# Two more tile pairs in a seven-product form, and its weight sums moved from VectorE to accumulating DMA

## The chip, the core and the metric

The kernel runs on one core of one Trainium2 chip. The metric is device time in microseconds of the whole launch. Three runs of the kernel before gave 1008.6, 1009.3 and 1009.34 us, so 1009.3 us is the median. One more run was profiled.

The engines have these names in the profile: PE is TensorE (matrix products; PEld is its weight load), DVE is VectorE (elementwise work), ACT is ScalarE (copies, casts and activation functions), POOL is GpSimd, which here issues DMAs and does little else, and SP is SyncE, which issues most of the weight loads.

## The reference

One layer of a decoder trunk over 512 tokens of width 1024, in float32. Cut to what matters here:

```python
h = rmsnorm(x, norm_mix_g)
proj = h @ w_in                       # 10 sections of 512 columns, then 3 x 1024 gate columns
...
branches = jnp.stack([conv_out, sb_out, ret_out], axis=2)
up = jnp.einsum('bsnw,nwd->bsnd', branches, w_branch)
gates = jax.nn.sigmoid(gate_logits.reshape(b, s, 3, 1024) + b_gate)
merged = jnp.sum(gates * up, axis=2)
x = x + merged @ w_o
```

After this come a cross-attention into 256 memory tokens and a squared-ReLU MLP, each with a residual add. The change is in `gates`: 24 tiles of 128 gate columns (three branches of eight), each a product of a 1024 x 128 block of `w_in` with the 1024 x 512 transpose of `h`.

## The kernel before

**Products.** Every float32 operand is split into a high and a low part (`parts_of` for weights, `split` for activations): the high part is a cast on ACT, the low part the difference to it, taken on DVE. Each product is then three matmuls, high by high, high by low and low by high (`mm3`, L362 to L364). A plain gate tile (`gates`, L1002) is 8 blocks of 128 rows by 3 matmuls of 512 columns, 24 in all. It is followed by the branch's own projection (`proj_t` with `nk=4`, 12 matmuls of 512 columns), a sigmoid on ACT and, on DVE, a multiplication and, for the second and third branch, an addition (`gated`, L986).

**The seven-product form** (`gates7`, `item_t7`, `seven`) takes two gate tiles at a time. Their weight, 1024 rows by 256 columns, is cut into four blocks B11, B12, B22 and B21 of 512 x 128. The activations are cut into four blocks by rows and token halves. Instead of eight block products with 512 rows and 256 tokens there are seven, of sums of blocks, as in the fast matrix multiplication of Strassen and Winograd. One product is 4 x 3 matmuls of 256 columns (L420), so a pair takes 84 matmuls of 256 columns instead of 48 of 512. The products use a PSUM bank several times over: `seven` runs A11·B11, S1·T1, S2·T2, A12·B21, S3·T3, S4·B22 and A22·T4 in this order, and between them copies partial results out on ACT (L426, L428, L430) or adds them on DVE (L432, L434, L436). So the third product waits until the first result has been copied out of its bank. S1 to S4 are sums of activation blocks, made once (`Mixes`); T1 to T4 are sums of weight blocks, made anew for each pair.

**Weights** stream through two rings. A load on SP's queue brings 128 x 1024 floats (512 KB) into one of six raw buffers (`w_raw`, `RAWS`). A *step* of a weight entry turns a raw buffer into high and low parts in `w_part`, ten buffers (`WBUFS`). Where a part has 512 columns, high and low share one buffer. A plain entry has one step. The class `Seven` has two loads, raw[0] with B11 | B12 and raw[1] with B22 | B21, and four steps: s0 makes the parts of B11; s1 forms T1 and T3 in place by two DVE operations of 512 columns (L129, L132) and makes their parts; s2 forms T2 and T4 by two more and makes theirs; s3 makes the parts of B22 and B21. This takes seven `w_part` buffers. `AHEAD = 2` steps are traced ahead of the item that needs them. The classes `Wide`, `Early` and `Summed` do the same for other matrices; two of them already let a DMA add one weight block to another (`add`, L235 to L237: a DMA of 512 KB issued by POOL, with `accum_op=ALU.add`).

**Order.** The kernel is traced as a list of items (`plan`). A planner then decides the order of instructions on each engine from costs that it assumes; at run time each engine takes its instructions in that fixed order, and waits come from semaphores. Only a few stretches keep the traced order.

**Which tiles.** `G7 = 12, G8 = 20`: of the 24 gate tiles, 12 to 19 are done in the seven-product form (two pairs of the second branch, two pairs of the third); the last four, tiles 4 to 7 of the third branch, are plain. Each two finished tiles of the third branch are made ready for the output projection on ACT and DVE by `Pairs.make` (L448). The output projection `w_o` follows (`items_w`, L494; steps of the class `Early`, which uses DVE for the sums of its stages P5 and P6 and one DMA add). Its stages P1, P2 and P5 come once for the first half of the merged tiles (j = 0) and once for the second (j = 1), then P6.

**Room for activations** is a pool of 30 units of 128 x 1024 floats. `Mixes` holds eight of them until the last seven-product pair has used them. The reload of `x` (L101, four units, issued on POOL in traced order) waits for free units.

Of the kernel before, what the change touches and what calls it, by code (L numbers as in the profile page):

```python
# [13 lines left out]
ALU = mybir.AluOpType  # L14

P = 128
# [15 lines left out]
C_N = 44  # L32
UNITS, SCRS = 30, 9
RAWS, WBUFS, AHEAD = 6, 10, 2
G7, G8, UP = 12, 20, 8


@with_exitstack
def trunk_kernel(ctx: ExitStack, tc: tile.TileContext, x, mem, par, rot, dqd, kdec, g_mix, g_xa, g_mem, g_mlp,
# [91 lines left out]
    def plus(out, a, b):  # L131
        dve.tensor_tensor(out=out, in0=a, in1=b, op=ALU.add)  # L132

# [43 lines left out]
    class Seven:  # L177

        def __init__(self, t, c):
            self.loads = [(t, c), (t, c + 1)]
            self.need = (1, 2, 2, 2)
            self.steps = [self.s0, self.s1, self.s2, self.s3]
            self.parts = []

        def s0(self, raw):
            return parts_of(raw[0][:, :512])

        def s1(self, raw):  # L190
            l, r = raw[0][:, :512], raw[0][:, 512:]
            minus(l, r, l)
            plus(r, r, raw[1][:, :512])
            return parts_of(raw[0])

        def s2(self, raw):
            l, r = raw[0][:, :512], raw[0][:, 512:]
            plus(l, raw[1][:, :512], l)
            minus(r, raw[1][:, 512:], l)
            return parts_of(raw[0])  # L200

        def s3(self, raw):
            return parts_of(raw[1])

        def get(self):
            where = dict(B11=(0, 0), T1=(1, 0), T3=(1, 1), T2=(2, 0), T4=(2, 1), B22=(3, 0), B21=(3, 1))
            return {n: [w[:, o * 512:(o + 1) * 512].rearrange("p (a b) -> p a b", a=4) for w in self.parts[i]]
                    for n, (i, o) in where.items()}

# [168 lines left out]
    class Mixes:  # L378
# [7 lines left out]
        def make(self, g):  # L386

            def whole(k0, t0):
                x = scr("mix", (P, 2, 256))
                hi, lo = self.a.span(k0 + 2 * g, 2, slice(t0, t0 + 256))  # L390
                dve.tensor_tensor(out=x, in0=hi.bitcast(F32), in1=lo.bitcast(F32), op=ALU.add)
                return x

            def mix(n, out, x, y, op):
                dve.tensor_tensor(out=out, in0=x, in1=y, op=op)
                h, l = self.parts[n]
                split(h[:, 2 * g:2 * g + 2, :], l[:, 2 * g:2 * g + 2, :], out)

            a11, a21 = whole(0, 0), whole(0, 256)
            mix("S3", scr("mix", (P, 2, 256)), a21, a11, ALU.subtract)  # L400
            mix("S1", a21, a21, whole(4, 256), ALU.subtract)
            mix("S2", a11, a11, a21, ALU.subtract)
            a12 = whole(4, 0)
            mix("S4", a12, a12, a11, ALU.subtract)

        def __getitem__(self, n):
            if n[0] == "S":
# [4 lines left out]
    def seven(b, a):  # L412


        def prod(ps, an, bn, first):
            bh, bl = b[bn]
            for k in range(4):
                ah, al = a[an][k]
                for i, (x, y) in enumerate(((bh, ah), (bh, al), (bl, ah))):
                    te.matmul(ps[:, :256], x[:, k, :], y, start=first and k == 0 and i == 0,  # L420
                              stop=k == 3 and i == 2, skip_group_check=True)

        p1, p2, p3 = atps("p1"), mmps("p2"), atps("p3")
        s, u = scr("sv_s"), scr("sv_u")
        prod(p1, "A11", "B11", True)
        act.copy(out=s[:, LH], in_=p1[:, LH])  # L426
# [7 lines left out]
        dve.tensor_tensor(out=s[:, RH_], in0=p1[:, LH], in1=s[:, RH_], op=ALU.add)  # L434
        prod(p3, "S4", "B22", False)
        dve.tensor_tensor(out=u[:, RH_], in0=p3[:, LH], in1=u[:, RH_], op=ALU.add)  # L436
        prod(p1, "A22", "T4", False)
        return s, u, p1

    class Pairs:  # L440
# [7 lines left out]
        def make(self, e, s, u):  # L448

            def put(names, src):  # L450
                w = unit("pr", (P, 2, 2, 256))
                split(w[:, 0], w[:, 1], src)
                for i, n in enumerate(names):
                    self.w[e][n] = w[:, 0, i, :], w[:, 1, i, :]

            def neg(out, a, b):
                dve.scalar_tensor_tensor(out=out, in0=a, scalar=-1.0, in1=b, op0=ALU.mult, op1=ALU.subtract)
# [1049 lines left out]
```

## Time and profile before

| | before |
|---|---|
| three runs | 1008.6, 1009.3, 1009.34 us |
| profiled execution | 1008.65 us, of which 1006.9 us span |
| mean granted TensorE clock | 0.997 of full speed |
| PE busy | 989.5 us, 98% of the span |
| DVE busy | 716.9 us, 71% |
| ACT busy | 531.2 us, 53% |
| POOL busy | 73.7 us, 7% |
| DMA | 113.61 MB, mean 113 GB/s |

In a line of groups the columns are line, engine, operation, output and inputs by the program's names, shapes, count, then busy time and the mean duration of one in ns, then the idle time of the engine just before and what ended it. Matmuls are pipelined: the duration of one is longer than the spacing of two, so what matters for PE is the spacing, which the chain of waits gives as a sum over many. The seven-product matmuls (L420) start between 373.1 and 443.6 us from the start of the span; those of the output projection (L494) begin at 468.2 us.

### The profile page before, as it was taken

How to read it: one execution, taken by the hardware profiler on the slowest of the kernel's cores; microseconds unless marked ns; L12 is line 12 of the kernel's file. 1: busy time of each engine (PE TensorE's matmuls, PEld its weight loads, DVE VectorE, ACT ScalarE, POOL GpSimd, SP SyncE). 2: the span in 40 equal slices, each digit the busy share in tenths (PEclk: the TensorE clock that was granted, in tenths of full speed). 3: DMA queues.
4: the chain of work that ended last, by engine and by line, in shares of the span. 5: the costliest groups of instructions: out<-in, count | busy, mean ns of one | idle time of the engine just before them, and what ended most of it. 6: DMA issues, size and time to landing. Idle time of an engine off the chain costs nothing.

```text
span 1006.9 us, 13109 instructions
## 1 busy us (share of the span) xinstructions
PE 989.5 (98%) x4944; PEld 836.9 (83%) x4944; DVE 716.9 (71%) x1073; ACT 531.2 (53%) x913; POOL 73.7 (7%) x136
## 2 busy tenths in 40 slices
PE   7999999999999999999999999999999999999997
PEld 6788888878888889988798888889888888888885
DVE  5757787778463797778896457875785785695786
ACT  6456666766533244454664446546643553553544
POOL 1000111223010000001100001010000000000000
PEclk9999999999999999999999999999999999999998
DMA  9342222222222213435565335733044035215212
GB/s 353 135 141 84 84 85 98 91 84 84 63 84 84 85 27 99 145 128 188 146 219 179 92 90 112 187 127 104 2 148 155 32 104 169 62 46 186 83 42 84
DMA packets 32352, 113.61 MB, mean 113 GB/s; under 512 B 4000, under 2 KB 4000, under 8 KB 32288
## 3 DMA queue, kind: packets, MB, share of 16 engines
q1 hardware_dynamic: 28224, 99.65, 29.9%
q0 software_dynamic: 3056, 11.02, 4.7%
q10 hardware_dynamic: 1008, 2.10, 0.6%
q8 instruction: 39, 0.64, 0.3%
q14 instruction: 25, 0.20, 0.1%
HBM read 110.66 MB, written 2.10 MB: 112 GB/s over the span
## 4 chain that ended last, share of the span: by engine, by line
PE 92%; DVE 3%; DMA 2%; issue 1%; ACT 1%; POOL 0%; SPq 0%; POOLq 0%; DVEq 0%
PE mm L362 21%; PE mm L363 21%; PE mm L364 21%; PE p L494 20%; PE p L420 4%; DVE w_part L114 1%; PE o L815 1%; DMA x<-in_x_dram 1%; PE aT L781 1%; DMA w_raw<-in_w_in_dram 1%; PE z L757 0%; PE z L758 0%; PE at L596 0%; PE xsc L363 0%; PE xsc L364 0%
## 5 line engine op out<-in xcount | busy, mean ns | idle before, releaser
L113 ACT CAST w_part<-w_raw 128x1024 fp32r<-128x1024 f32 (+1 forms) x223 | 232.4, 1045 | 275.9 <-PE mm L363 128.9
L114 DVE TENSOR_TENSOR w_part<-w_raw,w_part 128x1024 fp32r<-128x1024 f32 (+1 forms) x223 | 269.9, 1213 | 143.9 <-ACT w_part L113 137.3
L362 PE MATMUL mm<-hT_h,w_part 128*128 128x512 f32 (+1 forms) x736 | 280.1, 383 | 1.8 <-DVE r_qk L878 1.2
L363 PE MATMUL mm<-hT_l,w_part 128*128 128x512 f32 (+1 forms) x736 | 280.8, 382 | 0.7 <-DVE hT_l L352 0.7
L364 PE MATMUL mm<-hT_h,w_part 128*128 128x512 f32 (+1 forms) x736 | 280.6, 382 | 0.0
L494 PE MATMUL p<-w_part,pr 128*128 128x512 f32 x864 | 201.9, 390 | 0.9 <-DVE w_part L114 0.4
L494 PEld LDWEIGHTS p<-w_part,pr 128*128 128x128 f32 x864 | 161.7, 188 | 36.2 <-DVE x L132 1.0
L362 PEld LDWEIGHTS mm<-hT_h,w_part 128*128 128x128 f32 x736 | 137.8, 188 | 28.0 <-DVE r_qk L878 1.9
L363 PEld LDWEIGHTS mm<-hT_l,w_part 128*128 128x128 f32 x736 | 138.6, 188 | 25.9 <-DVE hT_l L352 1.0
L364 PEld LDWEIGHTS mm<-hT_h,w_part 128*128 128x128 f32 x736 | 138.5, 188 | 25.7
L132 DVE TENSOR_TENSOR w_raw<-w_raw 128x1024 f32<-128x1024 f32 (+1 forms) x46 | 51.8, 1127 | 2.2 <-DMA w_raw<-in_w_o_dram 1.9
L129 DVE TENSOR_TENSOR x<-x,p 128x512 f32<-128x512 f32 x48 | 32.5, 683 | 12.1 <-PE p L494 12.0
L494 PE MATMUL p<-w_part,pr_b 128*128 128x512 f32 x144 | 34.8, 389 | 0.0
L769 DVE TENSOR_TENSOR_SCAN sb_suf<-ones,sb_e 128x128 f32<-128x128 f32 (+3 forms) x32 | 27.4, 857 | 9.6 <-POOL sb_e L748 8.3
L132 DVE TENSOR_TENSOR x<-x,p 128x512 f32<-128x512 f32 x36 | 24.0, 683 | 12.9 <-PE p L494 12.8
L494 PEld LDWEIGHTS p<-w_part,pr_b 128*128 128x128 f32 x144 | 27.0, 188 | 5.6
L772 ACT ACTIVATE sb_suf<-sb_suf 128x128 f32<-128x128 f32 (+3 forms) x32 | 15.1, 471 | 29.7 <-DVE sb_suf L771 29.5
L420 PE MATMUL p<-mix_h,w_part 128*128 128x256 f32 x128 | 25.0, 283 | 0.0
L565 ACT ACTIVATE xn<-x 128x512 f32<-128x512 f32 x24 | 15.1, 629 | 13.1 <-DVE x L129 6.1
L362 PE MATMUL mm<-w_part,xg_h 128*128 128x512 f32 x56 | 21.4, 391 | 0.6 <-DVE sb_v L357 0.6
L363 PE MATMUL mm<-w_part,xg_h 128*128 128x512 f32 x56 | 21.8, 389 | 0.0
L364 PE MATMUL mm<-w_part,xg_l 128*128 128x512 f32 x56 | 21.5, 389 | 0.0
(257 smaller groups left out, 1447.4 us busy)
## 6 DMA issues: line engine op xcount, KB each, us to landing
w_raw<-in_w_in_dram SPq DMA_DIRECT2D x55, 512.0 KB, 3.4
w_raw<-in_w_up_dram SPq DMA_DIRECT2D x32, 512.0 KB, 3.5
w_raw<-in_w_down_dram SPq DMA_DIRECT2D x32, 512.0 KB, 3.7
w_raw<-in_w_br_dram SPq DMA_DIRECT2D x12, 512.0 KB, 3.4
w_raw<-in_w_gate_dram SPq DMA_DIRECT2D x8, 512.0 KB, 3.3
w_raw<-in_w_o_dram SPq DMA_DIRECT2D x8, 512.0 KB, 4.2
w_raw<-in_w_xk_dram SPq DMA_DIRECT2D x8, 512.0 KB, 4.9
w_raw<-in_w_xv_dram SPq DMA_DIRECT2D x8, 512.0 KB, 4.0
```

What stands on the lines that cost most here:

```text
L113: act.copy(out=wh, in_=src)
L114: dve.tensor_tensor(out=wl, in0=src, in1=wh.bitcast(F32), op=ALU.subtract)
L129: dve.tensor_tensor(out=out, in0=a, in1=b, op=ALU.subtract)
L132: dve.tensor_tensor(out=out, in0=a, in1=b, op=ALU.add)
L362: te.matmul(ps, lh, rh, start=first, stop=False)
L363: te.matmul(ps, lh, rl, start=False, stop=False)
L364: te.matmul(ps, ll, rh, start=False, stop=last)
L420: te.matmul(ps[:, :256], x[:, k, :], y, start=first and k == 0 and i == 0, stop=k == 3 and i == 2, skip_group_check=True)
L494: te.matmul(acc[bank, i], x, y, start=p in ("P1", "P5", "P2") and j + k + m == 0, stop=j == 1 and k == 1 and m == 2, skip_group_check=True)
L565: act.activation(out=dst[:, cs], in_=src[:, cs], func=AF.Square, accum_out=ss[:, i:i + 1])
L769: dve.tensor_tensor_scan(out=suf[:, :s][:, ::-1], data0=ones[:, :s], data1=e1[:, :s][:, ::-1], initial=0.0, op0=ALU.mult, op1=ALU.add)
L772: act.activation(out=suf[:, :s], in_=suf[:, :s], func=AF.Exp)
```

## The change

The boundary `G8` goes from 20 to 24, so tiles 20 to 23 are done as two more pairs in the seven-product form: six pairs instead of four, and the host lays out these columns of `w_in` accordingly. In `Seven`, the four DVE operations that form T1 to T4 are replaced by four accumulating DMAs of 256 KB each, which POOL issues and which read the second block from HBM again. All T are plain sums now: T1 = B11 + B12, T3 = B12 + B22, T2 = T1 + B22, T4 = T2 + B21. So the signs of the activation sums and of two recombinations change; some subtractions and additions become a `scalar_tensor_tensor` that computes -a - b (`neg`). T2 and T4 are now made one after the other, so their parts are two steps of 512 columns instead of one of 1024; there are five steps, with the same seven buffers.

```diff
-G7, G8, UP = 12, 20, 8
+G7, G8, UP = 12, 24, 8
...
+    def neg(out, a, b):
+
+        dve.scalar_tensor_tensor(out=out, in0=a, scalar=-1.0, in1=b, op0=ALU.mult, op1=ALU.subtract)
...
         def __init__(self, t, c):
+            self.t, self.c = t, c
             self.loads = [(t, c), (t, c + 1)]
-            self.need = (1, 2, 2, 2)
-            self.steps = [self.s0, self.s1, self.s2, self.s3]
+            self.need = (1, 1, 1, 2, 2)
+            self.steps = [self.s0, self.s1, self.s2, self.s3, self.s4]
             self.parts = []
 
+        def add(self, raw, side, i, from_side):
+            cols = lambda h: slice(512 * h, 512 * h + 512)
+            pool.dma_start(out=raw[0][:, cols(side)], in_=self.t[self.c + i][:, cols(from_side)], accum_op=ALU.add)
+
         def s0(self, raw):
-            return parts_of(raw[0][:, :512])
+            parts = parts_of(raw[0][:, :512])
+            self.add(raw, 0, 0, 1)
+            self.add(raw, 1, 1, 0)
+            return parts
 
         def s1(self, raw):
-            l, r = raw[0][:, :512], raw[0][:, 512:]
-            minus(l, r, l)
-            plus(r, r, raw[1][:, :512])
-            return parts_of(raw[0])
+            parts = parts_of(raw[0])
+            self.add(raw, 0, 1, 0)
+            return parts
 
         def s2(self, raw):
-            l, r = raw[0][:, :512], raw[0][:, 512:]
-            plus(l, raw[1][:, :512], l)
-            minus(r, raw[1][:, 512:], l)
-            return parts_of(raw[0])
+            parts = parts_of(raw[0][:, :512])
+            self.add(raw, 0, 1, 1)
+            return parts
 
         def s3(self, raw):
             return parts_of(raw[1])
 
+        def s4(self, raw):
+            return parts_of(raw[0][:, :512])
+
         def get(self):
-            where = dict(B11=(0, 0), T1=(1, 0), T3=(1, 1), T2=(2, 0), T4=(2, 1), B22=(3, 0), B21=(3, 1))
+            where = dict(B11=(0, 0), T1=(1, 0), T3=(1, 1), T2=(2, 0), B22=(3, 0), B21=(3, 1), T4=(4, 0))
...
             a11, a21 = whole(0, 0), whole(0, 256)
-            mix("S3", scr("mix", (P, 2, 256)), a21, a11, ALU.subtract)
-            mix("S1", a21, a21, whole(4, 256), ALU.subtract)
-            mix("S2", a11, a11, a21, ALU.subtract)
+            mix("S3", scr("mix", (P, 2, 256)), a11, a21, minus)
+            mix("S1", a21, whole(4, 256), a21, minus)
+            mix("S2", a11, a11, a21, neg)
             a12 = whole(4, 0)
-            mix("S4", a12, a12, a11, ALU.subtract)
+            mix("S4", a12, a12, a11, neg)
...
         prod(p1, "S3", "T3", False)
-        dve.tensor_tensor(out=s[:, RH_], in0=p1[:, LH], in1=s[:, RH_], op=ALU.add)
+        neg(s[:, RH_], p1[:, LH], s[:, RH_])
         prod(p3, "S4", "B22", False)
-        dve.tensor_tensor(out=u[:, RH_], in0=p3[:, LH], in1=u[:, RH_], op=ALU.add)
+        neg(u[:, RH_], p3[:, LH], u[:, RH_])
```

More of the change, by code (lines that the diff above doesn't have):

```diff
@@ L394, in mix @@
             def mix(n, out, x, y, op):
-                dve.tensor_tensor(out=out, in0=x, in1=y, op=op)
+                op(out, x, y)
                 h, l = self.parts[n]
@@ L454, in put @@
                     self.w[e][n] = w[:, 0, i, :], w[:, 1, i, :]
-            def neg(out, a, b):
-                dve.scalar_tensor_tensor(out=out, in0=a, scalar=-1.0, in1=b, op0=ALU.mult, op1=ALU.subtract)
             v = scr("pr_v", (P, 2, 256))
```

## The prediction

> **What bounds the kernel now.** I read the page's totals first, then the chain that ended last.
>
> ```profile
> span 1006.9 us, 13109 instructions
> PE 989.5 (98%) x4944; PEld 836.9 (83%) x4944; DVE 716.9 (71%) x1073; ACT 531.2 (53%) x913; POOL 73.7 (7%) x136
> PE 92%; DVE 3%; DMA 2%; issue 1%; ACT 1%; POOL 0%; SPq 0%; POOLq 0%; DVEq 0%
> ```
>
> PE is busy for 98% of the span and makes up 92% of the chain. A saving elsewhere shows only where PE waits. The profiled execution took 1008.65 us, 1.75 us more than its span; the median of the three runs is 1009.3, 0.65 above it.
>
> Then the view of busy time by stretches, from where the last two pairs of the third branch begin to the output projection (columns: us, then PE, PEld, DVE, ACT and POOL, clock, DMA share, GB/s).
>
> ```profile
> 403.00:418.00 15.00, 15.00 (x108) 14.12 (x107) 10.48 (x15) 6.58 (x11) 0.00 (x0) 1.00 0.36 105
> 418.00:433.00 15.00, 15.00 (x93) 13.53 (x92) 12.38 (x18) 7.00 (x12) 0.00 (x0) 1.00 0.43 141
> 433.00:448.00 15.00, 15.00 (x87) 13.21 (x86) 8.71 (x12) 6.67 (x11) 0.75 (x1) 1.00 0.59 190
> 448.00:458.00 10.00, 10.00 (x46) 8.29 (x45) 9.84 (x15) 5.25 (x8) 0.56 (x1) 1.00 0.34 120
> 458.00:468.00 10.00, 10.00 (x45) 8.27 (x45) 7.95 (x11) 4.51 (x8) 3.75 (x7) 1.00 0.54 179
> 468.00:478.00 10.00, 10.00 (x46) 8.27 (x45) 9.31 (x12) 5.55 (x7) 0.00 (x0) 1.00 0.54 206
> 478.00:488.00 10.00, 9.91 (x44) 7.89 (x43) 9.91 (x14) 3.88 (x5) 2.33 (x3) 1.00 0.71 142
> ```
>
> PE has no gap before 478 us, the clock is full, and the DMA share stays under 0.75. DVE is the second limit, but only from 448 us on: 9.84 + 7.95 + 9.31 + 9.91 = 37.0 us of 40, so 3.0 us are free. In the 15 us before, 6.3 are free. The waits of the weight load between 366 and 520 us say what that does:
>
> ```profile
> PEld p L494 <- DVE w_part L114: 0.8, 1, 0.8
> PEld p L494 <- DVE x L129: 0.5, 1, 0.5
> PEld p L494 <- DVE x L132: 0.5, 1, 0.5
> PEld p L494 <- ACT w_part L113: 0.5, 1, 0.5
> ```
>
> All are in the output projection (L494), three of four end on DVE. The one on L132 is at 484.8 us; the others, 1.8 us together, lie behind 495 us. So the gate stage is bound by PE alone, and the handover to the output projection by PE and DVE together.
>
> **The change part by part. (1) Matmuls.** The spacing comes from the chain in order of time:
>
> ```profile
> 377.54 5.74 PE p L420 x48
> 442.47 1.43 PE p L420 x12
> 468.41 8.17 PE p L494 x36
> ```
>
> 256 columns cost 5.74/48 = 119.6 ns, 512 columns 8.17/36 = 226.9 ns. A pair of plain tiles is 48 x 226.9 = 10.89 us, a pair in seven products 84 x 119.6 = 10.05 us. That saves 0.85 us a pair and **1.7 us** for the two new pairs. Seven eighths of the arithmetic would have saved 1.36 a pair, but the smaller matmul costs 5% more per column. The four older pairs keep their matmuls, so they gain nothing on PE. (The Trainium skill, "TensorE: Matmul & The Clock Gate", section "Back-to-back issue gap", gives N/2.4 + 2.5 ns for a warm clock. An estimate by it is 109 and 216 ns, which would save 2.4 us in all. The trace does not agree: it has 119.6 and 226.9 ns for the same thing, so the measurement decides and the rule gets no chance of its own.)
>
> **(2) VectorE and ScalarE.** Groups between 373.3 and 403 us, kept apart by shape:
>
> ```profile
> L114 DVE TENSOR_TENSOR w_part<-w_raw,w_part 128x1024 fp32r<-128x1024 f32 x9 | 11.0, 1220 | 2.9 <-ACT w_part L113 2.8 <-PE mm L363 0.2
> L129 DVE TENSOR_TENSOR w_raw<-w_raw 128x512 f32<-128x512 f32 x4 | 2.8, 690 | 0.1
> L132 DVE TENSOR_TENSOR w_raw<-w_raw 128x512 f32<-128x512 f32 x4 | 2.7, 686 | 0.1
> L114 DVE TENSOR_TENSOR w_part<-w_raw,w_part 128x512 fp32r<-128x512 f32 x2 | 1.4, 684 | 0.0
> L434 DVE TENSOR_TENSOR sv_s<-p,sv_s 128x256 f32<-128x256 f32 x2 | 0.8, 422 | 1.1 <-PE p L420 1.1
> L113 ACT CAST w_part<-w_raw 128x1024 fp32r<-128x1024 f32 x9 | 9.2, 1048 | 3.6 <-DVE w_raw L129 3.0 <-PE mm L364 0.6
> L113 ACT CAST w_part<-w_raw 128x512 fp32r<-128x512 f32 x2 | 1.2, 617 | 0.0
> L426 ACT COPY sv_s<-p 128x256 f32<-128x256 f32 x2 | 0.8, 375 | 0.7 <-PE p L420 0.6
> ```
>
> An old pair costs DVE 2 x 0.690 + 2 x 0.686 for the sums, 0.684 + 3 x 1.220 for the parts: 7.1 us. In the new form it is 3 x 0.684 + 2 x 1.220 = 4.5, so 2.6 us less. That buys nothing, since PE does not wait on DVE there. A new pair replaces two plain parts (2.44) by 4.5 and adds three recombinations of 0.42: **3.3 us more**, and these fall where DVE is scarce. On ACT a new pair costs about 3 us more (casts 3 x 0.617 + 2 x 1.048 instead of 2.10, three copies of 0.375); ACT is at most 56% busy in those stretches, which hides it.
>
> The `neg` form costs nothing: the same operation in `Pairs.make` takes 420 ns on 256 columns, against 422 for the addition that it replaces (L434). The four of 512 columns in `Mixes` cost at most 0.06 us more each by the second row, far ahead of the crowded stretch.
>
> ```profile
> L457 DVE SCALAR_TENSOR_TENSOR mg<-mg,pr_v x4: 418/420/424, 427.8 to 474.7; 128x256 f32<-128x256 f32 x4
> L855 DVE SCALAR_TENSOR_TENSOR cv_c<-cv_u,prm,cv_c 128x512 f32<-128x512 f32 x8 | 6.0, 747 | 0.1
> ```
>
> **(3) The accumulating DMAs.** The trace has adds of 512 KB (issue group and time to landing, minimum, median, maximum), plain loads, and transfers of 256 KB:
>
> ```profile
> L237 POOL DMA_DIRECT2D w_raw<-in_w_xo_dram x8: 856/860/976, 575.7 to 638.7; - x8
> DMA to landing us min/median/max: 5.2/5.4/8.1
> w_raw<-in_w_gate_dram SPq DMA_DIRECT2D x8, 512.0 KB, 3.3
> w_raw<-in_w_in_dram SPq DMA_DIRECT2D x2, 256.0 KB, 4.1
> out_dram<-xn SPq DMA_DIRECT2D x4, 256.0 KB, 2.6
> ```
>
> Twenty-four issues of 0.86 us are 21 us on POOL, which is idle between 403 and 433 us. An add of 256 KB was not measured: below, 2.6 us (a plain transfer of that size); above, 8.1 (the slowest add of twice the size). I take 4.6: 2.6 plus the 2 us by which a 512 KB add exceeds a plain load. (The Trainium skill, "DMA: Bandwidth & Descriptors", section "Anatomy of one DMA — SWDGE (gpsimd) path", fits 2.0 us + bytes/436 GB/s. That is an estimate of 2.6 us here, but also 3.2 for 512 KB, where the trace has 5.2 at least, so I do not use it; by it the slower rival below would lose half its chance.)
>
> Is that hidden? Ten `w_part` buffers hold nine for a pair and its branch, so s1 of the next pair starts when the fifth product has released T1 and T3. From there T2 needs s1 (1.05 + 1.22), an add (4.6) and s2 (0.62 + 0.68): 8.2 us. PE meanwhile has products 6 and 7 (2.9 us at 1.43 each), 24 branch matmuls (5.4) and the next pair's first two products (2.9): 11.2 us, 3.0 to spare. T4 needs another add and 1.3: 14.1 us against 11.2 + four products = 16.9, 2.8 to spare. With 2.6 us both are comfortable. With 8.1, T2 is 0.5 late and T4 4.2, though the planner may put branch matmuls ahead, as it does now. On average it is hidden; I price it at 0 and keep the upper end for the range.
>
> **(4) The handover.** The new pairs hold nine `w_part` buffers until late, so the parts of P2 and P5, now made from 451 us on, move some 5 us later, into the crowded stretch. The current deadline, in DVE's order of time:
>
> ```profile
> 482.34 0.69 DVE L352 TENSOR_TENSOR pr<-mg,pr 128x512 fp32r<-128x512 f32 x1
> 482.94 1.22 DVE L114 TENSOR_TENSOR w_part<-w_raw,w_part 128x1024 fp32r<-128x1024 f32 x1
> 484.08 2.00 DVE L132 TENSOR_TENSOR x<-x,p 128x512 f32<-128x512 f32 x3
> ```
>
> DVE finishes the parts and the `x` addition of this stage just as PE asks for them. The last new pair adds 3.3 us there, PE wants the result 1.7 us earlier, and 3.0 us are free: up to 2.0 us of new wait, and none if the planner uses the 6.3 free us before 448. I take the middle, 1.0 us.
>
> `Mixes` keeps eight units longer, and `x` waits for units:
>
> ```profile
> 461.68 1.07 POOL L101 DMA_DIRECT2D x<-in_x_dram  x2 [6.95 <-PE mm L364]
> ```
>
> `Mixes` is released product by product in the last pair, so these loads can still be issued before 468 us and are first wanted at 484.08. I price that at nothing; 16 us of distance cover it.
>
> **Sum:** -1.7 + 0 + 1.0 = -0.7 us. From the profiled run that is 1007.95, from the median 1008.6; I give 1008.3 us.
>
> **The rivals. Slower: ScalarE stands still behind an accumulating DMA.** The cast of s1, s2 and s4 now waits for a landing, and ACT takes its instructions in order. Queued behind are L426 and L430, which empty the bank that products 3 and 5 need, and the sigmoids. Such a wait exists already:
>
> ```profile
> 621.99 0.58 ACT L351 CAST xpT<-xpp 128x512 fp32r<-128x512 f32 x1
> 625.82 1.05 ACT L113 CAST w_part<-w_raw 128x1024 fp32r<-128x1024 f32 x1 [3.25 <-DMA w_raw<-in_w_xo_dram]
> 626.78 0.58 ACT L351 CAST xpT<-xpp 128x512 fp32r<-128x512 f32 x1
> ```
>
> ACT stood for 3.25 us with a cast queued behind. In the seven-product stage only one product, 1.43 us, lies between a result and the reuse of its bank; less the copy of 0.375 this covers 1.06 us, so such a wait costs PE 2.2 us. It decides from 1.06 us on: one hit eats the gain, two make it slower (+2.7). With 18 such casts, three hits are plausible: -1.7 + 6.6 = +4.9, about 1014 us; four, 1016. For it: the chain has under 3 us to spare and the planner's costs are assumed ones. Against: of ten adds only one was waited for in this way. Chance 0.25.
>
> **The adds do not get out in time.** POOL also works in order. If the planner puts an add of the last pair behind an `x` load that waits for a unit (6.95 us above), T4 is late by 6.95 - 2.8 = 4.1 us: +2.4 to +4, 1011.5 to 1013 us. Then the sums have not become free, only moved into a wait. Chance 0.06; against it, the adds come first in traced order.
>
> **Faster.** DVE has room after all, the 0.5 us wait at 484.8 goes too, and part of the 1.8 us behind 495 with it: -1.7 - 0.5 - 0.6 = -2.8, about 1006 us. For it: 2.6 us of DVE work goes away in each older pair. Against: that relief lies before 448 us, where nobody waits. Chance 0.21.
>
> **How the numbers follow.** The forecast has 0.48; its own range goes from 1006.8 (all of 1.7 kept, on the profiled run) to 1009.6 (2.0 us of wait, on the median). Two us, 0.2%, is about what a measurement of this kernel can tell from no change, and the gain on PE alone stays below it: hence faster 0.21 (the third rival), same 0.48 (the forecast), slower 0.31 (the first two). The range of 8 in 10 reaches from the faster rival at 1006 to just above three hits, 1014.5.
>
> **What would show it.** Right: 504 matmuls on L420 at 120 ns; L494 begins near 466.5 us; no sums of 512 columns on L129 and L132 with `w_raw`; 24 adds landing after some 4.6 us; no PE wait before 480 us; one on DVE near 483, longer than 0.5 us. Wrong: ACT waiting on a DMA of `w_gate` with PE waiting behind it on L426 or L430; DVE's share below 90% from 448 us on; or another spacing of L420, by which the 1.7 us falls.

## The result and the profile after

| | before | after |
|---|---|---|
| median of the runs compared | 1009.1 us (1008.6 to 1009.34) | 1046.8 us (1043.0 to 1049.1) |
| ratio, 95% interval | | 1.037 (1.0356 to 1.0385) |
| profiled execution, its span | 1008.65, 1006.9 us | 1049.09, 1047.4 us |

The change makes the kernel 37.7 us slower; forecast were 1008.3 us and a range to 1014.5. (After the change these line numbers are higher: the products of the seven-product form stand at L429, the output projection at L500, the copies of partial results at L435, L437 and L439, the accumulating DMA at L190.)

The page after: the span, the totals, and the row of the granted clock in 40 slices of 26 us.

```profile
span 1047.4 us, 13339 instructions
...
PE 1003.1 (96%) x5016; PEld 850.6 (81%) x5016; DVE 713.4 (68%) x1073; ACT 536.1 (51%) x933; POOL 94.9 (9%) x160
...
PEclk9999999999999998888989999999999999999999
```

DVE has become no busier (713.4 us against 716.9), and ACT only by 5 us. PE shows 13.6 us more of busy time, although the change saves it 1.7 us of matmuls at the full rate, and slices 16 to 19 and 21 have a clock below full. Next, the stretches that the prediction read, with the same columns, and their sum from 403 to 528 us:

```profile
403.00:418.00 15.00, 13.63 (x94) 12.51 (x93) 4.75 (x7) 5.23 (x10) 1.74 (x3) 0.99 0.40 80
418.00:433.00 15.00, 13.96 (x93) 12.58 (x91) 5.58 (x10) 5.27 (x9) 1.73 (x2) 1.00 0.64 157
433.00:448.00 15.00, 9.30 (x56) 8.43 (x56) 11.33 (x19) 7.49 (x15) 2.59 (x3) 0.77 0.43 107
448.00:458.00 10.00, 10.00 (x66) 9.04 (x65) 3.87 (x6) 2.38 (x4) 1.73 (x2) 1.00 0.52 104
458.00:468.00 10.00, 6.17 (x28) 5.84 (x28) 6.26 (x11) 5.56 (x11) 0.86 (x1) 0.66 0.51 107
468.00:478.00 10.00, 10.00 (x63) 9.01 (x63) 3.52 (x6) 2.55 (x5) 0.86 (x1) 1.00 0.52 131
478.00:488.00 10.00, 5.24 (x31) 4.55 (x31) 7.83 (x12) 4.36 (x9) 1.73 (x2) 0.86 0.24 40
...
518.00:528.00 10.00, 4.76 (x14) 3.19 (x13) 9.17 (x12) 4.40 (x5) 2.32 (x3) 0.74 0.70 131
sum 125.00, PE 102.04 PEld 90.16 DVE 74.59 ACT 49.79 POOL 18.32; mean PE 9.28 PEld 8.20 DVE 6.78 ACT 4.53 POOL 1.67
```

Before the change PE had no break from 403 to 478 us, by the rows in the prediction, and was busy for 9.91 of the ten us behind. Now it stands still for 125.00 - 102.04 = 23.0 us, 19.5 of them in the rows from 433, 458, 478 and 518 us. DVE is not what is busy instead: it has 3.5 to 7.8 us of ten between 448 and 488. In the same four rows the clock is at 0.66 to 0.86: the trace has five pieces of 6.83 us at half the clock. Four of them begin inside a gap of PE of 3.8 to 5.1 us, and the first begins at 396.41 us, just ahead of a gap of 2.9 us and behind two shorter ones. PE works in 25.1 us of these pieces, with 213 ns from one matmul of 256 columns to the next instead of 119.6, so some 11 us are lost by the rate. Idle time (23.0 us, and 5.0 more between 373 and 403 us) and lost rate make 39 us, near the 40.5 us between the spans of the two profiled executions; which of the two is a cause is not to be seen here, and an experiment decides it below.

What PE waited for between 360 and 530 us (total, times, longest):

```profile
PE p L429 <- ACT w_part L113: 15.8, 6, 4.4
PE p L500 <- DVE x L132: 5.1, 1, 5.1
PE mm L371 <- ACT w_part L113: 3.5, 2, 2.9
PE p L429 <- DVE w_part L114: 1.9, 3, 0.8
PE p L500 <- DVE w_part L114: 1.0, 1, 1.0
PE p L429 <- ACT sv_s L435: 0.5, 1, 0.5
```

In the pairs (L429 and L371) 19.3 of 21.7 us end on the cast of a weight part (L113), and only 0.5 us on a copy of a partial result (L435). And the group of the accumulating DMAs, with who waited for them:

```profile
L190 POOL DMA_DIRECT2D w_raw<-in_w_gate_dram x24: 863/863/1057, 322.2 to 485.7; - x24
...
who waited for it (us, times):
  ACT w_part L113: 52.2, 15
...
DMA to landing us min/median/max: 3.6/4.3/7.1
```

ACT stood 15 times for a landing, 52.2 us in all. The start of each pair's first product, and of the first matmul of the output projection, from the timelines (us; with six pairs the output projection's first matmuls stand in PE's order inside the last pair):

| kernel | pair 1 | 2 | 3 | 4 | 5 | 6 | output projection |
|---|---|---|---|---|---|---|---|
| before | 373.3 | 388.9 | 404.4 | 420.0 | | | 468.2 |
| after | 373.9 | 389.5 | 412.5 | 430.6 | 455.0 | 477.6 | 499.9 |
| six pairs, sums on DVE | 373.3 | 388.8 | 404.4 | 420.0 | 435.5 | 451.0 | 458.8 |
| after, s0 early | 373.4 | 389.7 | 405.6 | 423.2 | 440.1 | 463.5 | 468.6 |
| after, one add deep | 373.8 | 389.3 | 405.3 | 422.0 | 438.0 | 457.0 | 464.8 |
| after, both | 374.3 | 390.1 | 405.7 | 421.2 | 436.8 | 452.3 | 463.0 |
| after, PE kept busy | 374.1 | 389.7 | 412.6 | 431.0 | 454.6 | 481.4 | 504.0 |

PE's own work for a pair is 15.5 us (84 x 119.6 ns and 24 x 226.9 ns), and before the change that is the distance. Afterwards it is 18 to 24 us from the second pair on.

**The chain that sets this distance** can be read from two timelines of the changed kernel. First POOL's issues of the adds (start, duration, then the idle time before and what ended it), from 423.50 to 448.25 us:

```profile
423.50 0.86 POOL L190 DMA_DIRECT2D w_raw<-in_w_gate_dram  x1 [5.72 <-DVE w_part L114]
424.59 0.87 POOL L190 DMA_DIRECT2D w_raw<-in_w_gate_dram  x1 [0.23 <-DVE w_part L114]
434.21 0.86 POOL L190 DMA_DIRECT2D w_raw<-in_w_gate_dram  x1 [8.76 <-DVE w_part L114]
439.89 0.86 POOL L190 DMA_DIRECT2D w_raw<-in_w_gate_dram  x1 [4.81 <-DVE w_part L114]
446.55 0.86 POOL L190 DMA_DIRECT2D w_raw<-in_w_gate_dram  x1 [5.80 <-DMA w_raw<-in_w_gate_dram]
448.25 0.86 POOL L190 DMA_DIRECT2D w_raw<-in_w_gate_dram  x1 [0.84 <-DVE w_part L114]
```

ACT's casts of `w_part` in the same time, and DVE's low part of B11 and SP's load of the branch weight at its start:

```profile
431.62 1.05 ACT L113 CAST w_part<-w_raw 128x1024 fp32r<-128x1024 f32 x1 [5.83 <-DMA w_raw<-in_w_gate_dram]
...
438.25 1.56 ACT L113 CAST w_part<-w_raw 128x512 fp32r<-128x512 f32 x2 [5.21 <-DMA w_raw<-in_w_gate_dram]
...
443.56 1.57 ACT L113 CAST w_part<-w_raw 128x512 fp32r<-128x512 f32 x2 [0.67 <-DMA w_raw<-in_w_gate_dram]
...
445.29 0.62 ACT L113 CAST w_part<-w_raw 128x512 fp32r<-128x512 f32 x1
...
453.99 1.05 ACT L113 CAST w_part<-w_raw 128x1024 fp32r<-128x1024 f32 x1 [3.81 <-DMA w_raw<-in_w_gate_dram]
```

```profile
423.62 0.68 DVE L114 TENSOR_TENSOR w_part<-w_raw,w_part 128x512 fp32r<-128x512 f32 x1
```

```profile
423.39 0.33 SPq L314 DMA_DIRECT2D w_raw<-in_w_br_dram  x1
```

The two adds of s0 do not leave together. That of T3 does not touch B11, and by the semaphores in the trace it leaves a whole pair ahead, as soon as its raw load has landed: the cast at 431.62 waits for the adds of 400.48 and 424.59, and the one at 453.99 for those of 423.50 and 448.25. So a pair's chain begins with the add of T1, which overwrites B11 and has to wait for its low part (423.62 on DVE).

This add goes out at 424.59, and the cast of T1 and T3 starts when it has landed, at 431.62 (7.0 us). The low part follows on DVE, and POOL issues the next add at 434.21 (2.6). It lands, and the cast of T2 starts at 438.25 (4.0). The third add goes out at 439.89 (1.6), T4 is cast at 443.56 (3.7). Only behind that cast, and that of the branch weight in the same row, stands s0 of the next pair at 445.29 (1.7), and when its low part has been taken, behind that of the branch weight on DVE, the next add of T1 leaves at 448.25 (3.0). The sum is 23.7 us for one pair, of which PE's work covers 15.5. No step overlaps another, because s0 of the next pair stands behind s4 of this one on ACT.

The add of T1 is the slow one in it. In pairs 2 to 6 it landed after 5.5 to 6.9 us; each time a load of 512 KB was under way (here the branch weight, from 423.39 us), and in all but the last pair the add of T3 for the next one. The ten adds of T2 and T4 in the same pairs, and the first pair's add of T1, went out with no other transfer under way, and landed after 3.6 to 4.6 us.

### The profile page after: what moved, and what is told of

It is laid out like the page before. It is cut to its first block, busy times and chain, and to the rows that moved or that the text cites. A ratio compares the mean times of both kernels' runs of the same rounds, so it can differ in the third digit from the quotient of the medians.

```text
span 1047.4 us, 13339 instructions
## 1 busy us (share of the span) xinstructions
PE 1003.1 (96%) x5016; PEld 850.6 (81%) x5016; DVE 713.4 (68%) x1073; ACT 536.1 (51%) x933; POOL 94.9 (9%) x160
## 4 chain that ended last, share of the span: by engine, by line
PE 48%; DVE 3%; DMA 2%; issue 1%; ACT 1%; POOL 0%; POOLq 0%; DVEq 0%; ACTq 0%
PE p L500 19%; PE mm L372 9%; PE mm L373 9%; PE mm L371 9%; DVE w_part L114 1%; PE p L429 1%; DMA w_raw<-in_w_gate_dram 1%; DMA w_raw<-in_w_o_dram 1%; ACT w_part L113 0%; PE at L602 0%; PE xsc L373 0%; PE xsc L372 0%; PE xsc L371 0%; PE xpp L1245 0%; DVE x L132 0%
## 5 line engine op out<-in xcount | busy, mean ns | idle before, releaser
L114 DVE TENSOR_TENSOR w_part<-w_raw,w_part 128x1024 fp32r<-128x1024 f32 x233 | 274.8, 1182 | 184.6 <-ACT w_part L113 183.8
L113 ACT CAST w_part<-w_raw 128x1024 fp32r<-128x1024 f32 x233 | 235.1, 1017 | 310.8 <-PE mm L372 124.2
L371 PE MATMUL mm<-hT_h,w_part 128*128 128x512 f32 (+1 forms) x704 | 267.7, 383 | 1.8 <-DVE r_qk L884 1.2
L372 PE MATMUL mm<-hT_l,w_part 128*128 128x512 f32 (+1 forms) x704 | 268.4, 382 | 0.7 <-DVE hT_l L361 0.7
L373 PE MATMUL mm<-hT_h,w_part 128*128 128x512 f32 (+1 forms) x704 | 268.2, 382 | 0.0
L500 PE MATMUL p<-w_part,pr 128*128 128x512 f32 x864 | 204.6, 393 | 6.4 <-DVE x L132 5.1
L500 PEld LDWEIGHTS p<-w_part,pr 128*128 128x128 f32 x864 | 163.2, 190 | 41.9 <-DVE x L132 6.1
L371 PEld LDWEIGHTS mm<-hT_h,w_part 128*128 128x128 f32 x704 | 131.8, 188 | 26.7 <-DVE r_qk L884 1.9
L132 DVE TENSOR_TENSOR w_raw<-w_raw 128x1024 f32<-128x1024 f32 x38 | 46.4, 1222 | 3.5 <-DMA w_raw<-in_w_o_dram 3.2
L429 PE MATMUL p<-hT_h,w_part 128*128 128x256 f32 x144 | 31.5, 305 | 16.0 <-ACT w_part L113 15.3
L429 PE MATMUL p<-mix_h,w_part 128*128 128x256 f32 x192 | 43.1, 310 | 2.2 <-DVE w_part L114 1.2
L429 PEld LDWEIGHTS p<-hT_h,w_part 128*128 128x128 f32 x144 | 25.7, 209 | 17.7 <-ACT w_part L113 16.3
L429 PEld LDWEIGHTS p<-mix_h,w_part 128*128 128x128 f32 x192 | 35.3, 217 | 4.1 <-DVE w_part L114 1.6
L500 PE MATMUL p<-w_part,pr_b 128*128 128x512 f32 x144 | 34.6, 389 | 0.0
L190 POOL DMA_DIRECT2D w_raw<-in_w_gate_dram x24 | 21.0, 877 | 139.3 <-DVE w_part L114 111.2
L500 PEld LDWEIGHTS p<-w_part,pr_b 128*128 128x128 f32 x144 | 27.0, 188 | 5.6
```

The lines of the kernel that those rows point to most:

```text
L113: act.copy(out=wh, in_=src)
L114: dve.tensor_tensor(out=wl, in0=src, in1=wh.bitcast(F32), op=ALU.subtract)
L190: pool.dma_start(out=raw[0][:, cols(side)], in_=self.t[self.c + i][:, cols(from_side)], accum_op=ALU.add)
L371: te.matmul(ps, lh, rh, start=first, stop=False)
L372: te.matmul(ps, lh, rl, start=False, stop=False)
L373: te.matmul(ps, ll, rh, start=False, stop=last)
```

## The experiments

All times are medians; the kernel before ran beside each group, at 1008.8 to 1009.1 us. The letters of the theories are those of each text.

| run | us | ratio to before, 95% |
|---|---|---|
| six pairs, sums on DVE | 1018.3 | 1.0094 (1.0079 to 1.0109) |
| four pairs, sums by DMA | 1026.7 | 1.0169 (1.0152 to 1.0186) |
| after, s0 early | 1029.0 | 1.0199 (1.0184 to 1.0214) |
| after, one add deep | 1022.7 | 1.0137 (1.0122 to 1.0152) |
| after, PE kept busy | 1051.9 | 1.0426 (1.0410 to 1.0442) |
| after, one add deep and s0 early | 1019.6 | 1.0102 (1.0086 to 1.0117) |
| five pairs, the new one last | 1014.7 | 1.0061 (1.0049 to 1.0074) |
| five pairs, the new one first | 1010.6 | 1.0015 (1.0006 to 1.0024) |
| six pairs, output projection's sums by DMA | 1015.3 | 1.0064 (1.0051 to 1.0078) |
| before, output projection's sums by DMA | 1012.7 | 1.0039 (1.0026 to 1.0051) |
| five pairs, 11 part buffers, 29 units | 1022.4 | 1.0137 (1.0123 to 1.0151) |
| before, 11 part buffers, 29 units | 1018.4 | 1.0094 (1.0080 to 1.0107) |
| six pairs, PE held | 1016.7 | 1.0076 (1.0064 to 1.0089) |
| five pairs, PE held | 1015.4 | 1.0062 (1.0049 to 1.0074) |
| after, short chain, PE held | 1018.4 | 1.0092 (1.0077 to 1.0108) |
| before, PE held | 1014.9 | 1.0060 (1.0047 to 1.0072) |
| five pairs, PE held, no copy | 1015.1 | 1.0066 (1.0053 to 1.0080) |
| before, PE held, no copy | 1010.1 | 1.0012 (1.0003 to 1.0021) |

### The two halves of the change

The kernel before with six pairs and its own sums, and the changed kernel with four pairs:

```diff
-G7, G8, UP = 12, 20, 8
+G7, G8, UP = 12, 24, 8
```

> Only the two more pairs (G8 = 24); the sums stay on VectorE and the signs are the old ones. Theory A (the weight chain: in the changed kernel a pair's steps and three adds follow one another for 23 us, against 15.5 us of matmuls, and the next pair's chain starts only after it): there are no adds, so the stage runs at 15.5 us a pair and the time is 1007 to 1009.5 us. Rival B (the two pairs more and the handover to the output projection cost the time): 1020 us or more.

```diff
-G7, G8, UP = 12, 24, 8
+G7, G8, UP = 12, 20, 8
```

> Only the adds by DMA; the two older boundaries (G8 = 20, four pairs) stay. Theory A: pair starts some 15.6, 23, 18 and 24 us apart as in the changed kernel, so about 19 us more than before for the four pairs: 1024 to 1032 us. Rival B: 1008 to 1011 us, since these pairs are the old ones.

Both halves lose. Two more pairs alone cost 9.2 us, between the two expectations: the pairs run 15.5 us apart with no wait of PE over 0.4 us, and what is lost lies behind them, at the output projection. The sums by DMA alone cost 17.6 us with four pairs, as the theory of the chain had it: pairs 3 and 4 start at 412.7 and 430.5 us, and once the output projection has begun nothing is added (18.7 us late at its start, 18.3 by the span). By difference the sums by DMA are worth 37.7 - 9.2 = 28.5 us in the whole change, over six pairs instead of four.

### Shortening the chain

The step s0 of the next pair before s4 of this one, so that its add of T1 goes out before ACT waits for the last add of this one:

```diff
+            for e, nxt in zip(pairs, pairs[1:]):
...
+                self.steps.insert(e.last - 1, self.steps.pop(own))
```

> The changed kernel, with one step moved: s0 of the next pair (the parts of B11, which lets its first add go) is traced before s4 of this pair instead of after it. Theory A: s0 and the first add (1.3 + 4 to 7 us) leave the chain between two pairs, 23 falls to about 16 to 17 us: 1010 to 1022 us. Rival C (ScalarE stands behind landings and so holds up the copies that empty PSUM banks, whatever the chain): the number of waits is the same, so 1035 us or more.

T1 and T3 by DMA, T2 and T4 summed by DVE, so that no add waits for another:

```diff
         def s1(self, raw):
-            parts = parts_of(raw[0])
-            self.add(raw, 0, 1, 0)
-            return parts
+            return parts_of(raw[0])
 
         def s2(self, raw):
-            parts = parts_of(raw[0][:, :512])
-            self.add(raw, 0, 1, 1)
-            return parts
+            l, r = raw[0][:, :512], raw[0][:, 512:]
+            plus(l, l, raw[1][:, :512])
+            plus(r, l, raw[1][:, 512:])
+            return parts_of(raw[0])
```

> The changed kernel, but only T1 and T3 are made by DMA; T2 and T4 are sums on VectorE again, as before. The chain has one add instead of three: 23 falls to about 13 us, less than the matmuls of a pair. Theory A: 1007.5 to 1013 us. Rival C: a third to a half of the waits stay, 1018 to 1028 us.

And both together:

> Six pairs, one add deep (T1 and T3 by DMA, T2 and T4 summed by VectorE, as in the run with one add deep) and the next pair's s0 moved ahead of this pair's last step (as in the run with s0 early). If the chain of adds explains all of the loss in the gate stage, both cures together leave nothing of it: gap-free pairs 15.5 to 16 us apart, and only the handover of six pairs remains, 1018 us (1016 to 1020). If something else of the DMA form costs time there (the traffic of the adds, the order of the engines), it stays at 1022 us or over.

Moving one step in the order, with the same 24 adds, brings 17.8 us back, and the pairs come 16 to 18 us apart up to the fifth. The time is above the 1022 us expected; the 9.2 us behind the pairs are in it, which that expectation did not contain. The other 10.8 us above six pairs with sums on DVE are still lost in the pairs: the sixth starts 12.5 us later than there. The adds themselves hardly changed. Who waited for them, and their landing, in this run:

```profile
  ACT w_part L113: 36.0, 15
...
DMA to landing us min/median/max: 3.6/4.0/6.3
```

Fifteen waits as before, of 36.0 us instead of 52.2, at a median landing of 4.0 us instead of 4.3: it was the order that made them expensive, more than the DMA. The run with one add deep gave 1022.7 us, in the range of its rival; of its loss of 13.6 us, 9.2 are again those of six pairs. With both cures it is 1019.6 us, as expected, 1.3 above six pairs with sums on DVE. So the chain explains the loss in the pairs, to 1 or 2 us. The three longest waits of PE are now, between 360 and 530 us:

```profile
PE p L504 <- ACT pr L364: 3.3, 1, 3.3
PE p L504 <- DVE x L132: 2.3, 1, 2.3
PE p L504 <- DVE sv_u L136: 1.0, 1, 1.0
```

All three are in the output projection (L504 here), whose first stage runs beside the last pair.

### Is the half clock a cause?

The changed kernel with 20 matmuls of 512 columns, whose result is not used, ahead of the third product in pairs 4 to 6:

```diff
+        for _ in range(busy):
+            x = S["hT"](0)[0]
+            te.matmul(p2, x[:, :P], x, start=True, stop=True, skip_group_check=True)
         prod(p1, "S2", "T2", False)
```

> The changed kernel with 20 matmuls of 512 columns (4.5 us), whose result is not used, between the second and third product of the last three pairs, where PE stood still for 4.0 to 4.6 us. Theory C (the half clock of 6.8 us after each of these gaps costs time of its own): the clock stays full there, three stretches of half clock go, 1046.8 - 10 = 1037 us (1034 to 1041). Rival P (the chain of casts and adds sets the pace, and what PE loses at half clock lies in its shadow): the products start as late as before, 1043 to 1049 us; where no gap was, 4.5 us can be added. In both, no granted clock under 0.9 in the windows from 430 to 490 us.

```profile
433.00:448.00 15.00, 12.98 (x79) 11.00 (x80) 11.08 (x19) 6.54 (x12) 3.20 (x4) 1.00 0.45 109
448.00:458.00 10.00, 9.45 (x59) 8.36 (x58) 3.04 (x6) 2.37 (x4) 1.06 (x2) 1.00 0.49 103
458.00:468.00 10.00, 6.74 (x36) 5.38 (x34) 4.89 (x8) 3.41 (x6) 0.93 (x2) 1.00 0.45 105
468.00:478.00 10.00, 9.56 (x52) 8.53 (x53) 5.21 (x11) 5.03 (x11) 0.86 (x1) 0.83 0.53 132
478.00:488.00 10.00, 10.00 (x63) 8.98 (x62) 5.12 (x7) 2.77 (x5) 1.73 (x2) 1.00 0.30 47
```

The clock stays at 1.00 from 433 to 468 us, where it was 0.66 and 0.77; a fall of 3.4 us remains at 468.85 us, which neither theory expected. The time is 1051.9 us, not 1037; it is 3 us above the rival's 1043 to 1049, which allowed up to 4.5 us where the added matmuls meet no gap. The third product of pair 4, which waits for T2, starts at 439.66 us; in the changed kernel it was 439.87. In pair 5 it is 462.81 against 461.88. With the clock full these products start no more than 0.2 us sooner, so what PE does at half rate there lies in the shadow of the chain, and to fill the gaps gives nothing back. The theory that the clock costs 10 us of its own falls: where the rate is not lost, PE waits instead.

### Behind the pairs: what a further pair costs

One more pair only, at the end (tiles 22 and 23 plain), or at the front (tiles 10 and 11), sums on DVE:

```diff
-G7, G8, UP = 12, 20, 8
+G7, G8, UP = 12, 22, 8
```

> Five pairs, the last two tiles plain, sums on VectorE as before. Theory H (the 9 us at the handover come from the last seven-product pair standing right before the output projection: both its tiles end together, so the chain seventh product, sigmoid, product with the branch, Pairs.make lies bare): nothing of it is here, only 0.85 us of PE go: 1008.3 us (1007.3 to 1009.0), no PE gap over 1 us between 470 and 495 us. Rival V (VectorE's work of each added pair, 3.3 us, is what is late, wherever the pair stands): half of the loss, 1009.1 - 0.85 + 5 = 1013 us (1011.5 to 1015).

```diff
-G7, G8, UP = 12, 20, 8
+G7, G8, UP = 10, 20, 8
```

> Five pairs as well, the new one at the front (tiles 10 and 11 of the second branch), so that the last four tiles are plain as before and the handover is left as it was. Theory H and rival V agree here: 0.85 us less, 1008.3 us (1007.3 to 1009.0); first product at 362 us instead of 373. If it is over 1010 us, making the activation sums two tiles earlier costs something that neither names.

Neither gains its 0.85 us. At the end a pair costs 5.9 us, by these waits of PE in the output projection:

```profile
PE p L494 <- DVE x L132: 4.1, 1, 4.1
PE p L494 <- ACT pr L351: 2.5, 1, 2.5
```

At the front it costs 1.8 us, and both theories had expected a gain: the output projection begins 2.0 us later than before (470.2 against 468.2), after three waits of PE's weight load of 0.5 to 0.6 us in the seven-product stage. The bare chain after the last product (theory H) is not the reason in the first of these runs, since its last tiles are plain.

Then, the sums of the output projection's weights by DMA (`kind=Summed` in `proj_norm`), with six pairs and on the kernel before:

> Six pairs with sums on VectorE (1018.3 us), and the output projection's weight sums by accumulating DMA instead of by VectorE (the class Summed in place of Early), so VectorE is relieved by four sums of 1024 columns, about 5 us, around the handover. Theory V (VectorE is full at the handover, 475 to 492 us, and what PE waits for is late because of it): 1010 to 1014 us. Theory H (the bare chain after the seventh product): 1016 to 1020 us, with gaps over 2 us near 482 and 490 us still there. Adds that land too late could make it slower, over 1020 us; then ScalarE waits on a DMA of w_o.

> The kernel before with the output projection's weight sums by accumulating DMA (Summed in place of Early). With six pairs this gave 3.0 us. If VectorE is what is scarce at the handover in the kernel before too, the waits of PE there, about 2 us, go: 1006.5 to 1008 us. If not, an add that lands late makes ScalarE and PE wait as it did with six pairs (5.6 us once): 1010 to 1015 us.

With six pairs this gives 3.0 us, between the two expectations, and puts one wait of 5.6 us of PE for a cast, from 481.56 us, in the place of two. The add that the cast needed had gone out at 470.03 us and landed only at 483.00; by then ACT was busy with the memory tokens, and the cast came at 486.09. (ACT's longest stand for an add, 6.1 us, ended at 494.14, when PE had work.) On the kernel before it loses 3.9 us: PE waits 2.4 us for a low part, whose cast had stood 2.2 us for an add that took 12.1 us to land, and which then stood behind work on the memory tokens on DVE. More room on DVE may be worth something, but in both kernels an add that lands late costs PE a wait.

An eleventh part buffer, paid for with one unit:

```diff
-UNITS, SCRS = 30, 9
-RAWS, WBUFS, AHEAD = 6, 10, 2
+UNITS, SCRS = 29, 9
+RAWS, WBUFS, AHEAD = 6, 11, 2
```

> Five pairs, the last two tiles plain (1014.7 us), with eleven w_part buffers instead of ten, paid for by one unit of 30. Theory R (the pair's nine w_part buffers hold back the parts of the output projection, and VectorE's work bunches behind): against its control, the kernel before with the same rings, the loss falls from 5.9 us to under 2. Rival V (VectorE has no room: 3.3 us more work, and it stands in order behind products that come late): the loss stays at 4 us or more.

> Control of the run before it: the kernel before with eleven w_part buffers and 29 units. Theory R: PE waited about 2 us in the handover of the kernel before, so 1007.5 to 1009.5 us; one unit less can cost something where many are held, then over 1010 us, and only the difference to the run with five pairs is read.

The control lost 9.5 us itself, so the difference of 4.0 us between the two says little: the runs do not decide whether the part buffers hold the work back. They do show how near its edge the kernel before stands: one unit less of 30, with one part buffer more, costs more than the further pair that is discussed here.

Holding PE's order in the last pair, so that its other matmuls come behind the seventh product:

```diff
+            hold = tc.manual_schedule(engines={te.engine}) if c == 10 else None
+            if hold:
+                hold.__enter__()
             s, u, p1 = seven(w, S["mix"])
...
+            if hold:
+                hold.__exit__(None, None, None)
```

> Six pairs, sums on VectorE (1018.3 us), with PE's order held in the last pair: its seven products without output-projection matmuls between them, so 24 branch matmuls and 24 output-projection matmuls (10.9 us) stand behind the seventh product instead of in front of it. Theory H (the bare chain from the seventh product to Pairs.make): the gaps of 3.4 and 2.7 us and the half clock behind them go, 1009.5 us (1008 to 1012). Rival V (VectorE's work, 3.3 us more per pair, is late by itself): the gap moves and stays, 1015 us or more.

> Five pairs, the last two tiles plain (1014.7 us), PE's order held in the last pair as in the run before. There PE took 6.9 us of other matmuls between the third and fourth product, and VectorE stood 3.9 us in order behind the sixth product's result. If that stand is what bunched VectorE's work: 1008.5 to 1010.5 us. If VectorE has no room for 3.3 us more in any order: 1013 us or more.

> Six pairs with one add deep and s0 early (1019.6 us), PE's order held in the last pair. Theory H: as with the sums on VectorE, 1009.5 us (1008 to 1012.5), VectorE's 1.4 us less per pair changes nothing more. Rival V: 1015 us or more.

> The kernel before with PE's order held in its last pair, as a control: its handover has some 2 us of waits. If holding alone helps, 1007 to 1008.5 us; if the other matmuls inside the pair were covering something, over 1010 us, and then the two runs with more pairs lose as much by it.

It brings 1.6 us with six pairs, 1.2 with the short chain (one add deep and s0 early), nothing with five, and costs the kernel before 6 us. Theory H falls. With five pairs the wait has moved: PE now waits only 0.6 us in the output projection, and it stands in the last pair, before the third product, for the copy that empties its bank:

```profile
PE p L420 <- ACT sv_s L426: 4.9, 1, 4.9
```

So the last runs make the first product twice there, which makes that copy needless:

```diff
-        act.copy(out=s[:, LH], in_=p1[:, LH])
+        if not twice:
+            act.copy(out=s[:, LH], in_=p1[:, LH])
...
-        prod(p2, "A12", "B21", True)
...
+        if twice:
+            prod(p2, "A11", "B11", True)
+        prod(p2, "A12", "B21", not twice)
```

> Five pairs, PE's order held in the last one (1015.4 us), and there the first product is made twice: once in the bank where the third product is added to it, once more in the bank of A12*B21, so the third product no longer waits for the copy L426, which is left out together with the sum L432. 12 matmuls more, 1.4 us. Theory O (the loss is that copy, standing on ScalarE behind the casts of the pair before): 1015.4 - 5.0 - 3.4 + 1.4 = 1008.4 us (1008 to 1010.5). Rival V (VectorE has no room for the fifth pair): the handover gives it back, 1012 us or more, with a wait on VectorE of over 2 us behind 478 us.

> The same on the kernel before with PE's order held (1014.9 us): theory O 1014.9 - 4.6 - 3.4 + 1.4 = 1008.3 us (1008 to 1010.5). Rival: the wait goes to the copy L430 or to the parts, 1012 us or more.

With four pairs it works: PE has no gap over 1 us left, and the 1010.1 us are 1.1 above the kernel before, no more than the 1.4 us of the additional product. With five pairs the wait moves once more, to the second copy:

```profile
PE p L420 <- ACT sv_u L431: 4.2, 1, 4.2
```

ACT's and DVE's timelines around it show a ring:

```profile
442.60 1.05 ACT L113 CAST w_part<-w_raw 128x1024 fp32r<-128x1024 f32 x1 [1.50 <-PE p L420]
...
446.26 0.62 ACT L351 CAST pr<-mg 128x512 fp32r<-128x512 f32 x1 [2.24 <-DVE mg L998]
...
447.05 0.38 ACT L431 COPY sv_u<-p 128x256 f32<-128x256 f32 x1
```

```profile
443.68 1.23 DVE L114 TENSOR_TENSOR w_part<-w_raw,w_part 128x1024 fp32r<-128x1024 f32 x1 [1.55 <-ACT w_part L113]
444.82 0.68 DVE L997 TENSOR_TENSOR gt<-mm,gt 128x512 f32<-128x512 f32 x1
445.54 0.69 DVE L998 TENSOR_TENSOR mg<-mg,gt 128x512 f32<-128x512 f32 x1
```

A product frees a part buffer and ACT casts into it (442.60); DVE takes the low part (443.68), and only then the gated product and sum (444.82, 445.54) that stand behind it; ACT waits 2.24 us for that sum with the cast of `pr`; behind that cast stands the copy (447.05), and for the copy waits PE. Three orders on PE gave 1014.7, 1015.4 and 1015.1 us, with the loss in three places. The six us therefore do not belong to one wait of PE. Two readings remain: the part buffers, nine of ten of them held by a pair, or VectorE's 3.3 us of additional work (whose theory named a wait of over 2 us on VectorE for the run with five pairs, and none came). No run here separates them.

## Why the prediction was wrong

**What bounds the kernel** was read rightly: PE alone bound the pairs, and relieving DVE in them bought nothing.

**(1) Matmuls: right in size, not in effect.** 504 matmuls at 120 ns where the clock is full, and with the sums on DVE six pairs 15.5 us apart. But the 1.7 us never reached the end of the kernel; even the one pair at the front lost 1.8.

**(2) VectorE and ScalarE: right.** `neg` takes 420 to 422 ns, the sums of T are gone, and a new pair's 3.3 us on DVE fall where it is scarce. What these cost is (4).

**(3) The accumulating DMAs: here it failed**, at "On average it is hidden; I price it at 0". The landing was estimated well in the middle: 4.6 us, measured 3.6, 4.3 and 7.1 (least, median, most), inside the bounds of 2.6 and 8.1. The working before it began too late in the chain: "From there T2 needs s1 (1.05 + 1.22), an add (4.6) and s2". It took s0 and its add of T1 to be done by then. They were not, since s0 stands behind s4 of the pair before on ACT: from the cast of T4 to the add of T1 it is 4.7 us, and this add, beside other DMAs, takes 7.0 more. That is another 11.7 us in a chain of 23.7 us, against 15.5 of cover. The 3 us to spare were those of one link. And since every pair starts where the last one ended, no lateness is made up: 28.5 us in all. The run with s0 early, with nothing else changed, gave 17.8 of them back, and the one with one add deep as well 27.3.

**(4) The handover: mis-sized.** It said up to 2.0 us of new wait, 1.0 in the middle. Six pairs with sums on DVE measure 9.2 us more than before, so with the 1.7 us of matmuls that they save the term is 10.9. "None if the planner uses the 6.3 free us before 448" did not come about: in the run with five pairs DVE stood 3.9 us for a product and 1.8 for a load of `w_o` between 440 and 470 us, and was busy without a break only after. That free time in one stretch can be used by work of the next was assumed, and is what failed; what held the work back is the open point above.

**The rivals.** "ScalarE stands still behind an accumulating DMA" was right in direction and in the engine, and had 0.25. It expected one to four such waits, priced at 2.2 us each through the copies behind them; there were 15, and PE lost 0.5 us on a copy and over 20 on the parts themselves. Of the signs named for "wrong", two came true: ACT waited on a DMA of `w_gate`, with PE behind it at the products instead of at the copies, and DVE's share fell to 54% between 448 and 488 us. The prediction had the number of waits as an accident (three of 18 late), where the chain made nearly every one late. "The adds do not get out in time" named POOL's order behind a load of `x`; POOL's rows above show it waiting for the low part on DVE, or for a raw load of a later pair. The faster rival (DVE has room after all) is contradicted by the runs with five pairs. The half clock was not in the prediction; it need not be in the sum, as the run with PE kept busy shows, but it would have been the first thing to see in the profile.

## What to carry to other kernels

A dependent chain is costed over one whole period, from a step to the same step of the next round, with every engine's order in it, and compared with the work that covers one period; a margin worked out from the middle of the chain says nothing. Before a sum is moved to an accumulating DMA, look what stands in order before the step that issues it and behind the one that waits for it: here one step moved in the order was worth 17.8 us. With PE 98% busy, the other engines' orders were tight here as well: each added pair, at either end, lost more than the 0.85 us of PE that it saved.

## What the hardware showed that was not expected

With every PE gap of 3.0 us or more between 300 and 560 us, in all the runs here, the granted clock went to one half for 3.4 or 6.8 us; the fall began inside the gap or at most 1.6 us behind it. Gaps of 1.5 to 2.9 us had it in some cases. With 256 columns the spacing was then 213 ns instead of 120. The Trainium skill, "TensorE: Matmul & The Clock Gate", section "Part 1: The HAM clock gate", gives a window of about 3.4 us after whose idleness the clock falls to half. The traces agree in the length of the falls, one or two such windows. They do not show that a whole window has to be idle: one fall of the changed kernel began 1.9 us into a gap (437.37 us, PE's work ended at 435.43), and in the run with s0 early one came behind a gap of 1.5 us (at 497.86 us).

In the changed kernel an add of 256 KB landed after 3.6 to 4.6 us where no other transfer was under way at its issue (T1 in the first pair, T2 and T4 in the later ones), and after 5.5 to 6.9 us where it left beside loads of 512 KB and mostly another add (T1 in pairs 2 to 6). The one of the last pair, beside a load of `w_o` and no other add, took 5.5 us; what the load and the second add each have in the rest was not tried.
